# Differential heads of a hybrid block: keys transposed two heads ahead, the last head's steps filled with four blocks' products, two low parts behind the sums, and the last squares summed by TensorE

## The chip, the cores and the metric

The kernel runs on one NeuronCore of one Trainium2 chip. The metric is device time in microseconds of one execution. A NeuronCore has a matrix engine (TensorE, PE in the profile; its weight loads are PEld), a vector engine (VectorE, DVE), a scalar engine (ScalarE, ACT), a general engine (GpSimd, POOL) and a queue engine that issues most transfers (SyncE, SP). Each works through its own list in order and waits for the others by semaphores. SBUF is the on-chip memory, PSUM the memory into which TensorE writes, in eight banks of 128 x 512 fp32.

## The reference

One layer of a streaming encoder on 512 tokens of 1024 features:

```python
h = rms_norm(x, attn_norm_g)
z = h @ w_in                                  # MLA latents | diff q | diff k | diff v
y_mla  = mla_group(...)                       # 8 heads x 64
y_diff = diff_group(...)                      # 4 heads x 128
x = x + concat([y_mla, y_diff], -1) @ w_out
x = x + conv_ffn(rms_norm(x, ffn_norm_g), w_gate, w_up, conv_w, conv_b, w_down)
gate = sigmoid(rms_norm(x, ple_norm_g) @ w_ple_gate)
x = x + gate * (p @ w_ple_proj)
```

A differential head has two softmaxes over 64 features each, with a block-causal mask by chunks of 64 tokens and a bias by distance:

```python
logits = einsum('bhqmd,bhmkd->bhmqk', qb, k_t) * scale + bias   # m = 0, 1; masked
probs  = softmax(logits)
attn   = probs[:, :, 0] - lam * probs[:, :, 1]
o      = rms_norm(attn @ v, out_g) * (1 - lam_init)
```

All arithmetic is fp32.

## The kernel before

**Three products for one.** TensorE multiplies in a reduced format here, so each fp32 operand is split into a high part and a low part, and a product is made of three: high x high, high x low, low x high (`mm3`, lines 152 to 157; in the profile these are the lines 155, 156 and 157). Splitting costs one cast on ScalarE (the high part) and one subtraction on VectorE (the low part) per tile: `split`, lines 180 to 187, for activations; `load_w`, lines 143 to 150, for weights, after a load on SyncE's queue into one of three "raw" buffers.

**Stages around the change.** The MLA heads come first, then the four differential heads (about 160 to 226 us), then the rest of the product with w_out and the sums of squares for the next norm (about 226 to 247 us), then the product p @ w_ple_proj (`pp_unit`, from 242 us on), the normed tokens, and the FFN.

**A differential head `h` in four steps `t`.** Step t works on the queries of tokens 128t to 128t+127. The loop over `dslots` (lines 767 to 782) writes TensorE's order by hand. In each step:
- `diff_logits` two steps ahead: two banks "lg", for m = 0 and 1. VectorE adds the bias and finds the extreme (line 675), ScalarE makes the exponentials and their sums (line 676), VectorE combines both (lines 680 to 682).
- in step 0 only, `diff_T(h + 1, 1)`: the keys of the next head are transposed by TensorE (four transposes, d1T), cast by ScalarE, subtracted by VectorE (`st`).
- `pump(n)`: n units of other work for TensorE, from the list `fill`. `FILL_DIFF` (line 63) says how many in each step of each head. A unit is six products of a block with w_out (two of its eight slices of 128 inputs; `wo_units`, lines 638 to 650). The blocks `b` = 0 to 7 are the eight groups of 128 output features. A block's sum stands in a bank "acc" until VectorE adds it to x (line 631). First come the four MLA slices of all blocks (16 units), then, from head 3 on, slices 4 and 5 (differential heads 0 and 1) of the blocks 0 to 3 (four units).
- `probs_T`: the probabilities are transposed (pTd) and copied by ScalarE (pt, line 541).
- `diff_pv` of the step before: the product with the values (line 690). After step 3 the head's output is squared, summed and scaled (lines 696 to 706: sqo and yd on ScalarE, sso and mo on VectorE, ro on POOL, yd on VectorE).
- in step 0, `diff_T(h + 1, 0)`: the queries of the next head (d0T).
- in step 2, `y_split` of the head before: its output is transposed (yT) and split into yh and yl, the operands of the w_out product.

**Banks.** `bank` gives a PSUM bank by a tag: two "acc", three "lg", two "tp", one "ob". A new user waits until the last reader of the bank's former content is done. All transposes of the heads use "tp".

**After the last head** (lines 783 to 900). Six blocks get what their slices up to 6 still need (lines 802 to 807: one slice for blocks 0 to 3, three for blocks 4 to 7), with the transposes of the last head (`y_split(7)`) ahead of the sixth. Then the loop at 890 adds slice 7 to each in the order 0, 4, 1, 5, 2, 6, 3, 7; the last two blocks are made whole there. Each block is added to x by VectorE and squared by ScalarE; `sums_of` (lines 874 to 885) adds the squares, those of the first four on POOL, the others on VectorE. `norm_r` (lines 909 to 916) sums over the 128 partitions by four products with a column of ones (nr, two passes each) and takes the root; `norm_b` spreads it. `pp_unit` 0 and 1 stand ahead of `norm_r` in TensorE's order, 2 and 3 between `norm_r` and `norm_b`, and 4 to 7 after it. The first token block of the FFN, `tokens`, needs the norm.

**Who sets the order.** TensorE's order is written out in the whole kernel. VectorE's, ScalarE's and POOL's is set by a planner up to line 847: it takes, by its own cost model, what is ready, earlier lines first. `issue_after` holds an instruction behind another one on the same engine: the subtractions of `pk` (line 798) and of the first FFN weights (`behind_head`, lines 833 to 840: wT and wA) stand behind the scaling of the last head. From line 848 on the order of these engines is written out too (`manual_schedule`).

Of the kernel before, what the change touches and what calls it, by code (L numbers as in the profile page):

```python
# [61 lines left out]
FILL_MLA = (1, 1, 1, 1)  # L62
FILL_DIFF = ((2, 1, 1, 1), (1, 1, 2, 1), (1, 2, 2, 1), (1, 1, 2, 2))

# [30 lines left out]
def hybrid_block(ctx: ExitStack, tc: tile.TileContext, a: dict, out: bass.AP):  # L95
# [539 lines left out]
    def wo_w(kq, dq):  # L635
        return load_w(a["w_out"][kq, dq], 1024, f"o{kq}{dq}")
# [14 lines left out]

    df = {}

# [58 lines left out]
    def load_x():  # L712
# [6 lines left out]
        lambda: diff_T(0, 1),  # L719
        lambda: (y_split(0, ymn[0], None, "acc"), y_split(1, ymn[1], None, "acc"), load_x()),  # L720
        lambda: y_split(2, ymn[2], None, "acc"),
# [41 lines left out]
    mla_pv(*slots[-1])  # L763
    diff_logits(0, 1)
    pump()
    y_split(3, ymn[3], None, "tp")
    for i, (h, t) in enumerate(dslots):
        if i + 2 < len(dslots):
            diff_logits(*dslots[i + 2])
        if h + 1 < DH and t == 0:  # L770
            diff_T(h + 1, 1)
        pump(FILL_DIFF[h][t])
        df["pt", h, t] = probs_T(df.pop(("pm", h, t)), t, f"d{h}{t}", True)
        if i:
            diff_pv(*dslots[i - 1])
        if h + 1 < DH and t == 0:
            diff_T(h + 1, 0)
        if h and t == 2:
            y_split(4 + h - 1, df["y", h - 1], ocol, "tp")
        if h and t == 3:  # L780
            if h == 2:
                fill.append(wo_units(1, range(2), 2))
    pump()
    diff_pv(*dslots[-1])
    pump(100)

    for dq in (2, 3):  # L790
        wo2[dq] = wo_w(1, dq)

# [6 lines left out]
    ptw, wpp = (pk[:, 0], pk[:, 1]), [(pk[:, 2], pk[:, 3])]  # L799
    order = (0, 4, 1, 5, 2, 6, 3, 7)  # L800
    early = {}
    for b in order[:6]:
        n = len(early)
        if n == 5:
            y_split(7, df["y", 3], ocol, "tp")
        early[b] = bank("acc" if n < 2 else "lg" if n < 5 else "tp", f"o3{b}")
        mm3(early[b], wo_blocks(6 if b < 4 else 4, 7, b, wo2[b // 2]), True, False)
    att.release()
# [24 lines left out]
    def behind_head(src, tag, name, bufs=1):  # L833

        h_, l_ = (ffn.tile([P, 1024], F32R, tag=tag + j, bufs=bufs, name=f"{tag}{j}{name}") for j in "hl")
        with tc.issue_after(df["copy"].ins):
            df["hi"] = S.copy(h_, src)
        with tc.issue_after(df["scale"].ins):
            df["lo"] = V.tensor_tensor(l_, src, _f32(h_), op=ALU.subtract)
        return h_, l_  # L840

    gu = lambda f, c0, c1: a["w_gu"][f][:, 512 * c0:512 * c1]
    rpp = raw_w(a["w_pp"][1], "rS", "pp1", bufs=3)
    W = {0: {0: behind_head(raw_w(gu(0, 0, 2), "rA", 0, bufs=2), "wA", 0, bufs=2)}}
    wpp.append(behind_head(rpp, "wT", "pp1"))

# [27 lines left out]
    def sums_of(b):  # L874
# [6 lines left out]
        elif 4 < i < 7:  # L881
            V.tensor_tensor(half, half, sq, op=ALU.add)
        elif i == 7:
            V.tensor_tensor(nrm["ss"], nrm["ss"], half, op=ALU.add)
            V.tensor_tensor(nrm["ss"], nrm["ss"], sq, op=ALU.add)

    held = ExitStack()
    for i in ("hi", "lo"):
        held.enter_context(tc.issue_after(df[i].ins))
    for b in order:  # L890
# [3 lines left out]
        else:  # L894
            ps = bank("tp" if b == 3 else "lg", f"o3{b}")
            mm3(ps, wo_blocks(6 if b < 4 else 4, 8, b, wo2[b // 2]), True, True)
        add_x(b, ps)
        sums_of(b)
        held.close()
    wts.release()  # L900

# [7 lines left out]
    def norm_r():  # L909

        ss, ps = nrm["ss"], bank("ob", "nr")
        for t in range(NT):
            TE.matmul(ps[:, t:t + 1], ss[:, tsl[t]], ones[:, :1], start=True, stop=True)
        r4 = sm.tile([P, NT], F32, tag="r4", name="r4")
# [94 lines left out]
    for b in range(2):  # L1009
        pp_unit(b)  # L1010
    norm_r()
    for b in range(2):
        pp_out(b)
# [426 lines left out]
```

## Time and profile before

| what | value |
|---|---|
| median of three runs | 655.68 us (654.13 to 655.93) |
| the profiled execution's own time | 655.36 us |
| its span, first to last instruction | 653.5 us |
| TensorE busy | 642.6 us, 98% of the span |
| VectorE busy | 475.3 us, 73% |
| ScalarE busy | 362.4 us, 55% |
| POOL busy | 57.0 us, 9% |
| mean granted clock of TensorE | 0.995 |

The span is what the trace shows; the execution's own time has 1.86 us more around it. In rows of the trace the form is: start (us), duration (us), engine, line of the kernel, operation, output <- inputs, shapes, number of instructions merged in the row; in brackets the idle time of the engine just before it and what ended that. Durations of products overlap: they are pipelined, so the distance from one start to the next is what one costs. In a row of waits the numbers are the total in us, how many times, and the longest. In a row of a stretch the busy times of PE, PEld, DVE, ACT and POOL follow each other with the number of instructions, then the granted clock of TensorE (1.00 is full), the share of the DMA engines, and GB/s.

### The profile page before, as it was taken

What the parts mean: (1) busy time and instruction counts of PE and PEld (TensorE: products, weight loads), DVE (VectorE), ACT (ScalarE), POOL (GpSimd) and SP (SyncE); (2) the same over time, 40 slices, a digit from 0 to 9 for tenths busy, and PEclk for the clock granted to TensorE, in tenths of its full rate; (3) what the DMA queues carried; (4) which work ended last, traced back from release to release, by engine and by line L of the source; (5) the groups of instructions that cost most, each with busy time, mean ns of one, the idle gap of its engine ahead of it and who ended that gap; (6) DMA issues with size and microseconds to landing.
All of it is one profiled execution on the core that took longest, in us unless ns stands there. A gap on an engine that the chain in (4) does not pass through costs nothing.

```text
span 653.5 us, 10266 instructions
## 1 busy us (share of the span) xinstructions
PE 642.6 (98%) x3932; PEld 569.8 (87%) x3932; DVE 475.3 (73%) x860; ACT 362.4 (55%) x631; POOL 57.0 (9%) x93
## 2 busy tenths in 40 slices
PE   9999999999998999999999999999999999999997
PEld 9988888888777787889999999999999999988886
DVE  6789587666877677888886767677767676759444
ACT  7787666457665445656554645554454545637211
POOL 1520040000000121000100000000001000000000
PEclk9999999999998999999999999999999999999999
DMA  8241224143110157536675646564646464542121
GB/s 308 89 162 46 84 82 161 66 135 123 33 34 2 64 178 241 150 93 172 173 207 136 182 114 178 119 190 128 179 112 178 114 177 113 178 129 62 35 80 49
DMA packets 29912, 82.63 MB, mean 126 GB/s; under 512 B 3100, under 2 KB 4124, under 8 KB 29736
## 3 DMA queue, kind: packets, MB, share of 16 engines
q1 hardware_dynamic: 23816, 69.17, 31.8%
q0 software_dynamic: 5616, 12.33, 10.8%
q8 instruction: 31, 0.51, 0.3%
q10 hardware_dynamic: 432, 0.49, 0.2%
q14 instruction: 17, 0.14, 0.1%
HBM read 77.77 MB, written 5.52 MB: 127 GB/s over the span
## 4 chain that ended last, share of the span: by engine, by line
PE 87%; DVE 6%; ACT 4%; DMA 1%; issue 1%; POOL 0%; ACTq 0%; POOLq 0%
PE dn L157 6%; PE dn L156 6%; PE dn L155 6%; PE gx L157 4%; PE gx L155 4%; PE gx L156 4%; PE g L155 4%; PE g L156 4%; PE g L157 4%; PE zd L155 3%; PE zd L157 3%; PE zd L156 3%; PE pg L155 2%; PE pg L157 2%; PE pg L156 2%; PE u L155 2%
## 5 line engine op out<-in xcount | busy, mean ns | idle before, releaser
L827 DVE TENSOR_TENSOR wSl<-rS,wSh 128x1024 fp32r<-128x1024 f32 x21 | 25.7, 1224 | 44.3 <-ACT wSh L823 44.2
L157 PE MATMUL dn<-ah,lo_dn 128*128 128x512 f32 x144 | 56.4, 392 | 0.0
L156 PE MATMUL dn<-al,hi_dn 128*128 128x512 f32 x144 | 56.3, 391 | 0.0
L155 PE MATMUL dn<-ah,hi_dn 128*128 128x512 f32 x144 | 56.0, 389 | 0.0
L944 POOL DMA_DIRECT2D rS<-in_w_gu x19 | 22.7, 1194 | 251.0 <-DVE cv L1111 138.9
L823 ACT CAST wSh<-rS 128x1024 fp32r<-128x1024 f32 x21 | 22.1, 1051 | 35.6 <-PE gy L156 35.3
L155 PE MATMUL zd<-hi_d,xh 128*128 128x512 f32 x96 | 39.3, 410 | 0.0
L156 PE MATMUL zd<-lo_d,xh 128*128 128x512 f32 x96 | 37.6, 391 | 0.0
L631 DVE TENSOR_TENSOR x<-x,dn 128x512 f32<-128x512 f32 x44 | 29.9, 679 | 6.3 <-PE dn L157 6.1
L827 DVE TENSOR_TENSOR wTl<-rA,wTh 128x1024 fp32r<-128x1024 f32 x19 | 23.3, 1225 | 14.0 <-ACT wTh L823 13.4
L573 ACT ACTIVATE pm<-ml,nm,rq 128x128 f32<-128x128 f32 (+3 forms) x32 | 19.7, 617 | 22.6 <-DVE nm L571 22.6
L157 PEld LDWEIGHTS dn<-ah,lo_dn 128*128 128x128 f32 x144 | 27.0, 188 | 5.7
L156 PEld LDWEIGHTS dn<-al,hi_dn 128*128 128x128 f32 x144 | 27.0, 188 | 5.3
L155 PEld LDWEIGHTS dn<-ah,hi_dn 128*128 128x128 f32 x144 | 27.1, 188 | 5.2
L155 PE MATMUL o<-yh,hi_o 128*128 128x512 f32 x64 | 27.7, 432 | 1.0 <-DVE x L631 1.0
L676 ACT ACTIVATE pmd<-pmd,nmd 128x128 f32<-128x128 f32 (+3 forms) x32 | 17.9, 559 | 17.7 <-DVE nmd L675 17.7
L823 ACT CAST wAh<-rA 128x1024 fp32r<-128x1024 f32 x21 | 22.0, 1050 | 9.7 <-DMA rA<-in_w_gu 9.4
L1114 ACT ACTIVATE cv<-cv 128x512 f32<-128x512 f32 x22 | 13.9, 631 | 23.9 <-DVE cv L1111 23.8
L570 DVE TENSOR_REDUCE nm<-ml 128x1 f32<-128x128 f32 (+3 forms) x32 | 15.6, 487 | 15.1 <-PE ml L157 15.1
L155 PE MATMUL g<-b2h,wAh 128*128 128x256 f32 (+1 forms) x88 | 26.4, 300 | 0.2 <-ACT g L1067 0.2
L156 PE MATMUL g<-b2l,wAh 128*128 128x256 f32 (+1 forms) x88 | 26.2, 297 | 0.0
L157 PE MATMUL g<-b2h,wAl 128*128 128x256 f32 (+1 forms) x88 | 26.2, 297 | 0.0
(467 smaller groups left out, 2226.8 us busy)
## 6 DMA issues: line engine op xcount, KB each, us to landing
rA<-in_w_gu SPq DMA_DIRECT2D x22, 512.0 KB, 3.8
rS<-in_w_gu SPq DMA_DIRECT2D x22, 512.0 KB, 3.6
rS<-in_w_gu POOLq DMA_DIRECT2D x19, 512.0 KB, 6.0
raw_dn<-in_w_down SPq DMA_DIRECT2D x18, 512.0 KB, 5.9
raw_d<-in_w_d SPq DMA_DIRECT2D x12, 512.0 KB, 3.7
r<-in_w_gu SPq DMA_DIRECT2D x19, 256.0 KB, 6.1
raw_o<-in_w_out SPq DMA_DIRECT2D x8, 512.0 KB, 3.7
rS_pg<-in_w_pg SPq DMA_DIRECT2D x6, 512.0 KB, 4.0
```

Source lines behind the costliest of these rows:

```text
L155: TE.matmul(ps, xh, wh, start=first and i == 0, stop=False, skip_group_check=again)
L156: TE.matmul(ps, xh, wl, start=False, stop=False, skip_group_check=again)
L157: TE.matmul(ps, xl, wh, start=False, stop=last and i == n - 1, skip_group_check=again)
L570: V.reduce_max(nm, ps[:, :n], axis=AX.X, negate=True)
L573: S.activation(pm[:, :n], ps[:, :n], AF.Exp, bias=nm, scale=r, accum_out=mla["ssum", h // 2][:, t, h % 2:h % 2 + 1])
L631: V.tensor_tensor(xb(b), xb(b), ps, op=ALU.add)
L676: S.activation(pm[:, :n], pm[:, :n], AF.Exp, bias=nm, scale=-1.0, accum_out=s0 if m == 0 else s1)
L823: S.copy(h_, src)
L827: V.tensor_tensor(l_, src, _f32(h_), op=ALU.subtract)
L944: nc.gpsimd.dma_start(sums[f].rearrange("p (i c) -> p i c", i=2), a["w_gu"][f][:, :2048].rearrange("p (i c) -> p i c", i=2)[:, :, :512], a ...
L1114: S.activation(cv, cv, AF.Silu)
```

## The change

- The keys of head h + 2 are transposed at the end of step 3 of head h; those of head 1 ahead of the first unit, before the loop.
- One unit of head 2 moves from step 2 to step 3. Head 3 pumps 2, 2, 2 and 1 units, and one more comes ahead of its last product. The four units more are slices 4 and 5 of the blocks 4 to 7 (`early_units`), in banks that stay open ("acc" for 4 and 5, "lg" for 6 and 7). The last two pieces of w_out are loaded there, not after the heads.
- After the last head, the blocks 4 to 7 get slice 6, then blocks 0, 1 and 2 are begun with slice 6, with `y_split(7)` behind block 0. The loop that adds slice 7 goes 4, 5, 6, 7, 0, 1, 2, 3; block 3 is made there, in a bank "acc".
- The transposed second MLA block goes through a bank "lg" and not "acc".
- The low parts of wT and wA (one subtraction of 128 x 1024 each on VectorE) are no longer behind the scaling of the last head: that of wT comes after the last sum of squares, that of wA after `norm_r`.
- The last block's squares are not added by VectorE: `norm_r` takes them in four more products with the column of ones, accumulated in the same place.

```diff
-FILL_DIFF = ((2, 1, 1, 1), (1, 1, 2, 1), (1, 2, 2, 1), (1, 1, 2, 2))
+FILL_DIFF = ((2, 1, 1, 1), (1, 1, 2, 1), (1, 2, 1, 1), (2, 2, 2, 1))
...
-    df = {}
+    df, early = {}, {}
+
+    def early_units():
+
+        for b in range(4, 8):
+            if b % 2 == 0:
+                wo2[b // 2] = wo_w(1, b // 2)
+            early[b] = bank("acc" if b < 6 else "lg", f"o3{b}")
+            mm3(early[b], wo_blocks(4, 6, b, wo2[b // 2]), True, False)
+            yield
...
-        lambda: (y_split(0, ymn[0], None, "acc"), y_split(1, ymn[1], None, "acc"), load_x()),
+        lambda: (y_split(0, ymn[0], None, "acc"), y_split(1, ymn[1], None, "lg"), load_x()),
...
     diff_logits(0, 1)
+    diff_T(1, 1)
     pump()
     y_split(3, ymn[3], None, "tp")
     for i, (h, t) in enumerate(dslots):
         if i + 2 < len(dslots):
             diff_logits(*dslots[i + 2])
-        if h + 1 < DH and t == 0:
-            diff_T(h + 1, 1)
         pump(FILL_DIFF[h][t])
         df["pt", h, t] = probs_T(df.pop(("pm", h, t)), t, f"d{h}{t}", True)
         if i:
             diff_pv(*dslots[i - 1])
         if h + 1 < DH and t == 0:
             diff_T(h + 1, 0)
+        if t == 3 and h + 2 < DH:
+            diff_T(h + 2, 1)
         if h and t == 2:
             y_split(4 + h - 1, df["y", h - 1], ocol, "tp")
         if h and t == 3:
             if h == 2:
                 fill.append(wo_units(1, range(2), 2))
+                fill.append(early_units())
     pump()
     diff_pv(*dslots[-1])
     pump(100)
...
-    for dq in (2, 3):
-        wo2[dq] = wo_w(1, dq)
...
-    order = (0, 4, 1, 5, 2, 6, 3, 7)
-    early = {}
-    for b in order[:6]:
-        n = len(early)
-        if n == 5:
+    order = (4, 5, 6, 7, 0, 1, 2, 3)
+    for b in order[:7]:
+        if b < 4:
+            early[b] = bank(("lg", "tp", "ob")[b], f"o3{b}")
+        mm3(early[b], wo_blocks(6, 7, b, wo2[b // 2]), b < 4, False)
+        if b == 0:
             y_split(7, df["y", 3], ocol, "tp")
-        early[b] = bank("acc" if n < 2 else "lg" if n < 5 else "tp", f"o3{b}")
-        mm3(early[b], wo_blocks(6 if b < 4 else 4, 7, b, wo2[b // 2]), True, False)
...
-        with tc.issue_after(df["scale"].ins):
-            df["lo"] = V.tensor_tensor(l_, src, _f32(h_), op=ALU.subtract)
-        return h_, l_
+        return h_, l_, src
...
-    W = {0: {0: behind_head(raw_w(gu(0, 0, 2), "rA", 0, bufs=2), "wA", 0, bufs=2)}}
-    wpp.append(behind_head(rpp, "wT", "pp1"))
+    wA0 = behind_head(raw_w(gu(0, 0, 2), "rA", 0, bufs=2), "wA", 0, bufs=2)
+    W = {0: {0: wA0[:2]}}
+    wT_ = behind_head(rpp, "wT", "pp1")
+    wpp.append(wT_[:2])
...
             V.tensor_tensor(nrm["ss"], nrm["ss"], half, op=ALU.add)
-            V.tensor_tensor(nrm["ss"], nrm["ss"], sq, op=ALU.add)
+            nrm["sq"] = sq
 
     held = ExitStack()
-    for i in ("hi", "lo"):
-        held.enter_context(tc.issue_after(df[i].ins))
+    held.enter_context(tc.issue_after(df["hi"].ins))
     for b in order:
         if b in early:
             ps = early[b]
             mm3(ps, wo_blocks(7, 8, b, wo2[b // 2]), False, True)
         else:
-            ps = bank("tp" if b == 3 else "lg", f"o3{b}")
-            mm3(ps, wo_blocks(6 if b < 4 else 4, 8, b, wo2[b // 2]), True, True)
+            ps = bank("acc", f"o3{b}")
+            mm3(ps, wo_blocks(6, 8, b, wo2[b // 2]), True, True)
         add_x(b, ps)
         sums_of(b)
         held.close()
+    lo_(*wT_)
...
         ss, ps = nrm["ss"], bank("ob", "nr")
+        ss = [ss] + ([nrm.pop("sq")] if "sq" in nrm else [])
         for t in range(NT):
-            TE.matmul(ps[:, t:t + 1], ss[:, tsl[t]], ones[:, :1], start=True, stop=True)
+            for i, s in enumerate(ss):
+                TE.matmul(ps[:, t:t + 1], s[:, tsl[t]], ones[:, :1], start=i == 0, stop=i == len(ss) - 1)
...
     for b in range(2):
         pp_unit(b)
     norm_r()
+    lo_(*wA0)
```

More of the change, by code (lines that the diff above doesn't have):

```diff
@@ L785, in hybrid_block @@
     pump(100)
-    for dq in (2, 3):
-        wo2[dq] = wo_w(1, dq)
+    assert len(early) == 4
     pk = kvp.tile([P, 4, 1024], F32R, tag="kv", name="pk")
```

## The prediction, made before the changed kernel ran

> **What bounds the kernel now.** I read first the page's busy times, then the waits of TensorE, then its order of time wherever it stood idle in the stretch that the diff touches (160 to 260 us), and last the engines it waited for.
>
> ```profile
> span 653.5 us, 10266 instructions
> PE 642.6 (98%) x3932; PEld 569.8 (87%) x3932; DVE 475.3 (73%) x860; ACT 362.4 (55%) x631; POOL 57.0 (9%) x93
> ```
>
> TensorE is busy for 642.6 of 653.5 us, and the diff takes no product away. So the change can only win idle time and slow clock of TensorE. The waits of TensorE between 150 and 265 us (total, times, longest):
>
> ```profile
> PE d0T L657 <- ACT pt L541: 1.7, 1, 1.7
> PE o L155 <- DVE x L631: 1.0, 1, 1.0
> PE yT L617 <- DVE st L184: 0.4, 1, 0.4
> PE nr L913 <- DVE nr L885: 0.4, 1, 0.4
> ```
>
> These four are all there is to win, with one addition, the clock. The stretches in which the longest wait lies and the two that follow (after the engines' busy times: granted clock, DMA share, GB/s), then TensorE's rows in order of time (start, duration):
>
> ```profile
> 198.00:200.00 2.00, 0.93 (x7) 0.73 (x9) 2.00 (x4) 2.00 (x5) 0.00 (x0) 1.00 0.00 0
> 200.00:202.00 2.00, 2.00 (x9) 1.35 (x6) 2.00 (x4) 0.58 (x1) 0.38 (x1) 0.61 0.00 0
> 202.00:204.00 2.00, 2.00 (x6) 1.56 (x5) 1.54 (x5) 0.00 (x1) 0.63 (x1) 0.54 0.00 0
> ```
>
> ```profile
> 199.07 0.66 PE L657 MATMUL d0T<-ident,zd 128*128 128x128 f32 x4 [1.69 <-ACT pt L541]
> ...
> 200.59 0.79 PE L155 MATMUL o<-yh,hi_o 128*128 128x512 f32 x1
> ...
> 204.04 0.39 PE L157 MATMUL o<-yh,lo_o 128*128 128x512 f32 x1
> ...
> 205.98 0.50 PE L155 MATMUL o<-yh,hi_o 128*128 128x512 f32 x1
> ...
> 207.94 0.40 PE L157 MATMUL o<-yh,lo_o 128*128 128x512 f32 x1
> ```
>
> After 1.69 us without work the clock fell to 0.61 and 0.54. From the row at 200.59 to the one at 204.04 it is eight products in 3.45 us; from 205.98 to 207.94 it is eight in 1.96 us. The slow clock cost 3.45 - 1.96 = 1.49 us. This one wait is therefore worth 1.69 + 1.49 = 3.18 us, more than the others together. The wait of 0.96 us at 220 us was followed by no fall.
>
> **Part 1: key transposes earlier.** ScalarE ahead of the wait:
>
> ```profile
> 192.61 1.05 ACT L796 CAST pk<-raw_pp 128x1024 fp32r<-128x1024 f32 x1 [0.53 <-DMA raw_pp<-in_w_pp]
> ...
> 197.35 0.56 ACT L183 CAST st<-d1T 128x512 fp32r<-128x512 f32 x1
> 197.81 1.04 ACT L148 CAST hi_o<-raw_o 128x1024 fp32r<-128x1024 f32 x1
> 198.76 0.26 ACT L541 COPY pt<-pTd 128x128 f32<-128x128 f32 x1
> ```
>
> The query transpose d0T of head 3 needs one of the two "tp" banks; the copy of pTd that frees it stood behind the cast of the keys d1T, whose bank was the other one, and behind a weight cast. The change issues the keys one step earlier (end of step 3 of the head before), so that bank is read out before d0T asks for it. Nothing is added: the same four transposes, cast and subtraction. The wait should go, and the clock with it: -3.18 us; bounds 0 (the weight cast at 197.81, 1.04 us long, still stands ahead of the copy that is needed) and -3.18. I take the whole, because d0T no longer needs the late bank. For head 1 the keys now go ahead of the transposes of the fourth MLA block, whose low part is used soon after; at the same place the second MLA block takes an "lg" bank, which aims at the 0.4 us wait on st. Gain and loss there are each bounded by that row, 0.4 us; I take 0.
>
> **Part 2: filling the last head.** Head 2 spreads its units so that step 3 has one, and head 3 gets seven units and an eighth ahead of its last product, where it had four. Products are moved, not added. Their weights cost nothing new: the loads of all eight w_out pieces were issued long before (below, SyncE's queue), ahead of the pT load as now, and the last cast of them is the row at 197.81. The cover is this distance of some 20 us to the units; without it a load and a cast would stand in the step.
>
> ```profile
> 144.95 11.95 SPq L140 DMA_DIRECT2D raw_o<-in_w_out  x3
> 175.61 0.33 SPq L140 DMA_DIRECT2D raw_pT<-in_pT  x1
> ```
>
> The wait to be won here, VectorE first, then TensorE:
>
> ```profile
> 219.30 0.69 DVE L706 TENSOR_TENSOR yd<-yd,ro 128x512 f32<-128x512 f32 x1 [0.57 <-POOL ro L704]
> 219.91 0.68 DVE L631 TENSOR_TENSOR x<-x,o 128x512 f32<-128x512 f32 x1
> ```
>
> ```profile
> 220.64 0.50 PE L155 MATMUL o<-yh,hi_o 128*128 128x512 f32 x1 [0.96 <-DVE x L631]
> ```
>
> A unit waited for its "acc" bank, whose addition stood in VectorE's queue behind the scaling that waited for POOL. Four w_out blocks and two of the new ones still go through the two "acc" banks, in steps 0 to 2. So it is between 0 and -0.96. I take -0.7, nearer to the row: the addition was late through one scaling in the queue, and in the new order the bank that is asked for at that time was filled a step earlier.
>
> **Part 3: what the moved products covered.** They stood behind the last head product and hid the chain that makes the last head's y. TensorE, ScalarE, VectorE in order of time:
>
> ```profile
> 225.67 0.48 PE L155 MATMUL o<-yh,hi_o 128*128 128x512 f32 x1
> ...
> 231.91 0.60 PE L617 MATMUL yT<-ident,yd 128*128 128x128 f32 x4
> 232.26 0.47 PE L155 MATMUL o<-yh,hi_o 128*128 128x512 f32 x1
> ```
>
> ```profile
> 232.54 0.69 ACT L186 ACTIVATE yh<-yT,ocol 128x512 fp32r<-128x512 f32 x1 [5.51 <-PE yT L617]
> ```
>
> ```profile
> 228.65 0.69 DVE L706 TENSOR_TENSOR yd<-yd,ro 128x512 f32<-128x512 f32 x1 [1.19 <-POOL ro L704]
> 229.26 1.22 DVE L798 TENSOR_TENSOR pk<-raw_pT,pk 128x1024 fp32r<-128x1024 f32 x1
> 230.39 1.22 DVE L798 TENSOR_TENSOR pk<-raw_pp,pk 128x1024 fp32r<-128x1024 f32 x1
> 233.27 0.75 DVE L187 SCALAR_TENSOR_TENSOR yh7l<-yT,ocol,yh 128x512 fp32r<-128x512 f32 x1 [1.66 <-ACT yh L186]
> ```
>
> The 27 products from 225.67 to 231.91 give 6.24 / 27 = 0.231 us each. y is ready at 228.65 + 0.69 = 229.34, 3.67 us after 225.67. The new order leaves 15 products, 3.47 us: +0.2 us of waiting. The transposes then run from about 229.4 and hold TensorE for 232.26 - 231.91 = 0.35 us; six products (1.39) follow, so the first product with yh7 comes at 231.14 and the one with its low part at 231.37. But VectorE is in the two pk subtractions until 230.39 + 1.22 = 231.61, and the low part takes 0.75 more: 232.36, a wait of 0.99. If the planner puts it between them it is ready 233.27 - 231.91 + 0.75 = 2.11 us after the transposes start, 231.51: a wait of 0.14. The pk subtractions come first in the program and are ready first; I take +0.8.
>
> **Part 4: the sums of squares.** The subtractions of wT and wA leave the front of this stretch, the last square goes to TensorE. VectorE, ScalarE, TensorE:
>
> ```profile
> 240.90 0.82 DVE L882 TENSOR_TENSOR nr<-nr,nsq 128x512 f32<-128x512 f32 x1 [0.75 <-ACT nsq L878]
> 241.64 0.67 DVE L631 TENSOR_TENSOR x<-x,o 128x512 f32<-128x512 f32 x1
> 243.08 0.69 DVE L882 TENSOR_TENSOR nr<-nr,nsq 128x512 f32<-128x512 f32 x1 [0.76 <-ACT nsq L878]
> 243.69 0.68 DVE L631 TENSOR_TENSOR x<-x,o 128x512 f32<-128x512 f32 x1
> ```
>
> ```profile
> 244.46 0.63 ACT L878 ACTIVATE nsq<-x 128x512 f32<-128x512 f32 x1 [1.42 <-DVE x L631]
> ```
>
> ```profile
> 245.12 0.39 PE L157 MATMUL pp<-pk 128*128 128x512 f32 x1
> 245.87 1.05 PE L913 MATMUL nr<-ones,nr 128*128 128x1 f32 x8 [0.37 <-DVE nr L885]
> 246.79 0.48 PE L155 MATMUL pp<-pk 128*128 128x512 f32 x1
> ```
>
> Here the order is written out, so each block goes: add, square on ScalarE, add of the square. From one such add to the next is 243.08 - 240.90 = 2.18 us, add to add of the square 243.08 - 241.64 = 1.44, add of the square to the next block's add 0.61 to 0.74. Let T be when TensorE leaves the sixth block; its add starts some 0.28 us later (the lag from 232.26 to 232.54). Then the square is added at T + 1.72, the seventh at T + 3.90, the eighth block's add starts at T + 4.51 and ends at T + 5.13, its square ends at T + 4.51 + 0.77 + 0.63 = T + 5.91. TensorE has after T now only the seventh block (3 products), the eighth (6) and pp0 (6): T + 3.47. And pp1 takes an "acc" bank: with two of them, and block 3 now in "acc" too, pp1's is block 3's, free at T + 5.13. TensorE waits 5.13 - 3.47 = 1.66 us, and behind pp1 are the norm's products and everything else of TensorE. Lower bound 1.2, if the sixth block's add is not behind. In exchange the norm's own wait goes, which is 245.87 - (245.12 + 0.23) = 0.52: net +1.14. The eight 128x1 passes take 246.79 - 245.87 = 0.92 us; sixteen cost +0.92, none of it hidden, since TensorE is the bound. The moved subtractions, 1.2 us each on VectorE, lie one behind the sums while TensorE does pp1, one behind the norm's scaling while TensorE does pp2 to pp7; without these products the second would delay the first token block by its 1.2 us.
>
> **Sum.** -3.18 + 0 - 0.7 + 0.2 + 0.8 + 1.14 + 0.92 = -0.82 us. The profiled run took 655.36 us, 1.86 more than its span; that gives 654.5. The runs' median is 655.68, 0.32 above the profiled run; I predict 654.7.
>
> **Rivals.** (a) *All waits of the heads go and the tail costs its lower bounds.* For it: the bounds are read off an order in which VectorE was late. Against: the written order forces the chain. -3.18 - 0.96 - 0.4 + 0.2 + 0.14 + (1.2 - 0.52) + 0.92 = -2.6: 652.9.
> (b) *The clock falls in the tail.* The wait for pp1's bank, 1.66 us, is as long as the 1.69 that cost 1.49 us, and the sixteen narrow passes follow. Against: 0.96 us at 220 us brought no fall, and the wait is shorter than the one that did. -0.82 + 1.49 = +0.67: 656.2.
> [...]
> (c) *Slower: the long wait stays.* Place: d0T of head 3. Mechanism: ScalarE runs in order and still waits for the raw_pp load (0.53 us at 192.61), casts it (1.05), and casts the weights (1.04) ahead of the copies and casts that free the two "tp" banks. [...] Then the 3.18 stay in: -0.82 + 3.18 = +2.36: 657.9. For it: those casts are untouched. Against: one of the three items in front of the copy, the key cast of 0.56 us, is gone, and the bank needed is another.
>
> **How the numbers follow.** Forecast 0.45, (a) 0.28, (b) 0.17, (c) 0.10. What a measurement can tell from no change is about 0.3%, 1.97 us: faster means under 653.7, slower over 657.65. Faster takes most of (a), 0.23, and 0.08 of the forecast: 0.31. Slower takes half of (c) and a little of (b): 0.08. Same 0.61. The range runs from a little below (a), where the first bounds all fall well, to a little above (b): 652.3 to 656.8; the forecast's own is 653.4 to 655.9.
>
> **What would show it.** Right: no 1.7 us wait of d0T and a full clock from 195 to 210 us; a wait of pp on VectorE's x (1.2 to 1.7 us) right before the norm; nr with sixteen passes and no wait; a wait of some 0.8 us on yh7l. Wrong: a PEclk below 1 in the stretch of the norm (b), a d0T that waits for pt or st (c), or a pp1 that starts with no wait, which would break my reading of the "acc" banks.

## The result and the profile after

The kernel with the change takes 662.18 us (661.63 to 662.46, median of 4), the kernel before 655.54 us beside it (654.13 to 655.93, median of 4). The ratio is 1.0101 with an interval of [1.0074, 1.0128]: some 6.6 us slower. The prediction was 654.7 us in a range of 652.3 to 656.8, with a chance of 0.08 for slower. It was wrong.

The profiled execution of after took 662.22 us. Its page begins:

```profile
span 660.4 us, 10291 instructions
PE 647.9 (98%) x3940; PEld 574.5 (87%) x3940; DVE 475.6 (72%) x859; ACT 363.0 (55%) x631; POOL 56.6 (9%) x93
```

TensorE has only eight instructions more, the eight narrow passes of the norm, but 5.3 us more of busy time (642.6 before), and its idle time rose from 10.9 to 12.5 us. Most of the loss is therefore time with products in it, slower ones above all. The waits of TensorE from 150 to 280 us in after (total, times, longest) show where the idle time went:

```profile
PE pp L155 <- DVE x L631: 2.8, 1, 2.8
PE pTm L538 <- ACT pm L573: 0.9, 1, 0.9
PE o L156 <- DVE yh7l L187: 0.6, 1, 0.6
PE dl L157 <- DVE st L187: 0.4, 1, 0.4
PE o L155 <- DVE x L631: 0.3, 1, 0.3
PE yT L617 <- DVE yd L715: 0.2, 1, 0.2
```

The wait of d0T (1.7 us before) is gone, as forecast. The largest wait is now the one for the bank of pp1, the second product of p @ w_ple_proj. The stretches of after around it (busy times of PE, PEld, DVE, ACT, POOL, then granted clock, DMA share, GB/s):

```profile
244.00:248.00 4.00, 1.24 (x6) 0.73 (x5) 3.25 (x5) 1.00 (x2) 0.35 (x1) 1.00 0.01 5
248.00:252.00 4.00, 4.00 (x20) 3.74 (x18) 1.28 (x2) 2.17 (x4) 0.00 (x0) 0.61 0.42 63
252.00:256.00 4.00, 4.00 (x13) 3.28 (x13) 2.18 (x4) 0.49 (x2) 2.28 (x2) 0.54 0.52 200
256.00:260.00 4.00, 4.00 (x17) 2.92 (x16) 3.64 (x5) 2.34 (x5) 0.00 (x0) 1.00 1.04 211
```

The clock falls behind that wait; 0.61 and 0.54 are means over 4 us. In before every stretch from 240 to 256 us had 1.00. TensorE in order of time, after (start, duration; in brackets the wait):

```profile
243.28 0.40 PE L155 MATMUL pp<-pk 128*128 128x512 f32 x1
...
247.59 0.50 PE L155 MATMUL pp<-pk 128*128 128x512 f32 x1 [2.76 <-DVE x L631]
...
248.62 0.40 PE L156 MATMUL pp<-pk 128*128 128x512 f32 x1
248.84 0.60 PE L157 MATMUL pp<-pk 128*128 128x512 f32 x1
249.24 0.42 PE L924 MATMUL nr<-ones,nr 128*128 128x1 f32 x2
...
252.51 0.77 PE L155 MATMUL pp<-pk 128*128 128x512 f32 x1
...
263.18 0.39 PE L155 MATMUL g<-b1h,wAh 128*128 128x512 f32 x1
```

The last product ahead of the norm's passes, at 248.84, is already slow: the next row comes 0.40 us later, where the one before had 0.22.

Call the time from the first product of pp0 to the first product g of the FFN the norm's stretch: 263.18 - 243.28 = 19.90 us here. In before the same two landmarks lie at 242.57 and 255.97 us: 13.40. This stretch alone lost 6.50 us; the heads ahead of it did not pay for it.

**What of the 6.9 us between the two spans is the change.** The order of instructions is the same in both kernels up to about 145 us, and yet in this profile the three issues of raw_o, the last common point, start at 147.38 us and not at 144.95. The 2.43 us arise at the start: the sixteen one-column passes ssx, sums for the first norm, begin 0.73 us later than in a later profile of the same kernel (20.73 against 20.00 us), and some 1.6 us more are lost behind them, where the clock fell. After's stretch, then the same stretch in that later profile (e13):

```profile
24.00:28.00 4.00, 4.00 (x16) 3.88 (x15) 3.00 (x14) 2.03 (x5) 3.08 (x8) 0.63 0.35 112
```

```profile
24.00:28.00 4.00, 4.00 (x22) 3.67 (x21) 3.61 (x24) 3.18 (x5) 3.12 (x12) 1.00 0.29 100
```

So this part belongs to the execution and not to the change. To separate the two, both kernels were profiled again, unchanged.

> The changed kernel once more. Theory 'chance at the start': the slow clock at 24 to 28 us and the first loads that land 0.9 us late are not of this program; some of these executions lack them and take 1.5 to 2.4 us less than 662.2. Rival 'of the program': all of them lie between 661.6 and 662.5 again. The slow clock behind the norm (249 to 255 us) should be in most of them.

It took 662.72 us (662.1 to 663.96, 4 executions), ratio 1.0107 [1.0088, 1.0126], and repeats the result.

> The changed kernel, one look. Chance: the first loads land early or late, and the clock at 20 to 28 us is 1.0 or about 0.65, independent of the program. Of the program: late loads and a slow clock at 24 to 28 us again, as in both looks so far. Behind the norm (248 to 256 us) the clock about 0.5 either way.

> As the look before it: the changed kernel once more, for the same question.

> The kernel before, one look. Chance: the start may show late loads and a slow clock at 24 to 28 us here too, and the slow clock behind d0T's wait at 200 us may be missing. Of the program: the start is at full clock, as in its one look so far.

> As the look before it: the kernel before once more, for the same question.

The change took 661.50 and 661.48 us, before 653.48 and 653.67 us, one execution each; in none of the four did the clock fall at the start. e13 (the change) and e14 (before) are compared here. TensorE's rows in order of time, e13 first:

```profile
240.92 0.40 PE L155 MATMUL pp<-pk 128*128 128x512 f32 x1
...
245.24 0.63 PE L155 MATMUL pp<-pk 128*128 128x512 f32 x1 [2.76 <-DVE x L631]
...
262.39 0.39 PE L155 MATMUL g<-b1h,wAh 128*128 128x512 f32 x1
```

```profile
241.02 0.40 PE L155 MATMUL pp<-pk 128*128 128x512 f32 x1
...
244.31 1.05 PE L913 MATMUL nr<-ones,nr 128*128 128x1 f32 x8 [0.36 <-DVE nr L885]
...
245.23 0.48 PE L155 MATMUL pp<-pk 128*128 128x512 f32 x1
...
254.41 0.39 PE L155 MATMUL g<-b1h,wAh 128*128 128x512 f32 x1
```

At pp0 the change is level with before (240.92 against 241.02). The norm's stretch takes 21.47 us against 13.39. The whole difference of the spans, 659.7 - 651.7 = 8.0 us, is made in this stretch, and e13 has the fall of the clock there as well. It begins with the first product behind the wait (the six of pp1 lie 0.43 us apart), 2.4 us ahead of the norm's first pass at 247.81:

```profile
242.04:245.45 3.41, 0.65 (x3) 0.21 (x3) 2.65 (x5) 0.80 (x2) 0.00 (x0) 1.00 0.00 0
245.45:248.86 3.41, 3.41 (x12) 2.83 (x11) 1.48 (x2) 2.47 (x4) 0.00 (x0) 0.50 0.36 25
```

For all kernels below, the norm's stretch from the starts of the same two products (us):

| profile | pp0 | first g | norm's stretch |
|---|---|---|---|
| before | 242.57 | 255.97 | 13.40 |
| before (e14) | 241.02 | 254.41 | 13.39 |
| after | 243.28 | 263.18 | 19.90 |
| after (e13) | 240.92 | 262.39 | 21.47 |
| e1, keys alone | 240.98 | 254.38 | 13.40 |
| e2, block 3 elsewhere | 243.36 | 262.45 | 19.09 |
| e3, VectorE adds the last squares | 240.80 | 256.92 | 16.12 |
| e4, keys as before | 243.74 | 265.19 | 21.45 |
| e5, more products ahead of the norm | 243.39 | 260.03 | 16.64 |
| e6, last squares alone | 241.49 | 255.17 | 13.68 |
| e7, keys, fill, wT | 239.35 | 252.58 | 13.23 |
| e8, low parts alone | 241.20 | 255.31 | 14.11 |
| e9, additions first | 240.96 | 255.48 | 14.52 |
| e10, without POOL's sums | 242.57 | 258.46 | 15.89 |

### The profile page after: what moved, and what is told of

Same layout as the page of the kernel before. It is cut to its first block, busy times and chain, and to the rows that moved or that the text cites. A ratio compares the mean times of both kernels' runs of the same rounds, so it can differ in the third digit from the quotient of the medians.

```text
span 660.4 us, 10291 instructions
## 1 busy us (share of the span) xinstructions
PE 647.9 (98%) x3940; PEld 574.5 (87%) x3940; DVE 475.6 (72%) x859; ACT 363.0 (55%) x631; POOL 56.6 (9%) x93
## 4 chain that ended last, share of the span: by engine, by line
PE 81%; DVE 8%; ACT 5%; DMA 3%; issue 2%; POOL 0%; ACTq 0%; POOLq 0%; DVEq 0%; SPq 0%
PE dn L157 6%; PE dn L156 6%; PE dn L155 6%; PE gx L157 4%; PE gx L155 4%; PE gx L156 4%; PE g L155 4%; PE g L157 4%; PE g L156 4%; PE zd L155 3%; PE zd L157 3%; PE zd L156 3%; PE pg L155 2%; PE pg L157 2%; PE pg L156 2%; PE u L156 2%
## 5 line engine op out<-in xcount | busy, mean ns | idle before, releaser
L836 DVE TENSOR_TENSOR wAl<-rA,wAh 128x1024 fp32r<-128x1024 f32 x22 | 26.8, 1217 | 1.2 <-ACT wAh L832 1.0
```

## The experiments

**The key transposes, alone on before (e1) and alone taken out of after (e4).** The edit of e1; e4 is the same edit undone:

```diff
     diff_logits(0, 1)
+    diff_T(1, 1)
     pump()
...
-        if h + 1 < DH and t == 0:
-            diff_T(h + 1, 1)
...
+        if t == 3 and h + 2 < DH:
+            diff_T(h + 2, 1)
```

> The kernel before with one part of the change alone: the key transposes two heads ahead. Theory 'tail' (the loss of the change sits behind the heads; this part wins): the 1.69 us wait of d0T and the slow clock behind it go, 655.5 - 3.2 = 652.3 us. Rival 'heads' (moving transposes only moves the wait, because ScalarE's order is replanned): within 0.5 us of 655.5, with a wait of about 1 to 2 us elsewhere between 160 and 225 us.

> The change with the key transposes where they were before. Theory 'tail': the keys are the part that wins, so without it d0T waits again for 1 to 1.7 us, and if the clock falls there too the time is 662.2 + 1.7 to 3.2 = 664 to 665.4 us. Rival 'heads': the same or less than 662.2 us. The start of the kernel (the first 150 us) has the same order of instructions in all of these kernels: if the slow clock at 24 to 28 us of the changed profile belongs to chance, some of them show it and some do not.

With the keys alone 653.61 us (653.32 to 655.74, 10 executions) against 654.72 (653.40 to 657.07, 13): ratio 0.999 [0.9979, 1.0001]. The wait of d0T is gone, but the gain is at most about 1.4 us by the interval, not 3.18. The other direction shows why: e4 (662.1 us, 1.0118 [1.0094, 1.0142]) has the wait again, and no fall of the clock behind it. Its wait, then its stretch:

```profile
PE d0T L666 <- ACT pt L541: 1.8, 1, 1.8
```

```profile
200.00:204.00 4.00, 2.53 (x15) 1.79 (x16) 3.93 (x9) 2.98 (x6) 0.00 (x0) 1.00 0.00 0
```

Before itself, in e14 and e15, has the wait of d0T (1.8 and 1.7 us) with a full clock behind it as well. Of six profiles with this wait (before, e4, e6, e8, e14, e15) only the one from which the prediction was made has the fall. It is not of the program. The executions of before beside e1 with a mean clock of 1.0 took 653.87 to 654.72 us, those with 0.995 took 654.93 to 657.07; where it was lower in these, a mean doesn't say.

The wait itself was not won whole either. From raw_o to pp0 e1 takes 95.51 us, the four profiles with before's order there and a full clock (e6, e8, e14, e15) 95.92 to 96.28: 0.4 to 0.8 us less, though a wait of 1.7 to 1.8 us is gone. The only new wait is one of 0.2 us (dl for st). What took the rest is open.

**The bank of pp1: block 3 elsewhere (e2).**

```diff
-            ps = bank("acc", f"o3{b}")
+            ps = bank("tp", f"o3{b}")
```

> The change with block 3 in a bank tp instead of acc, so that pp1 need not wait for block 3's addition. Theory 'bank': the 2.76 us wait of pp1 goes and the clock stays up: 662.2 - 2.8 - 3 = about 656.5 us. Rival 'chain of sums': TensorE comes to the norm's passes at about 246.1 us on the time axis of the changed profile, while the last square ends at 248.3; a wait of about 2.2 us stands there instead, and the time falls by only 0.5 us, to about 661.7, with the slow clock still there.

658.55 us (657.43 to 661.55, 4), 1.0068 [1.0041, 1.0095]. The wait of pp1 is gone, so the bank was read rightly. But TensorE then waits at the norm, for the same chain of sums:

```profile
PE nr L924 <- DVE nr L893: 2.0, 1, 2.0
```

```profile
248.00:252.00 4.00, 3.72 (x17) 3.72 (x18) 1.52 (x3) 2.26 (x4) 0.03 (x1) 0.56 0.41 58
```

The bank only decides where the wait stands; VectorE's chain of additions and sums is what is late. The clock falls here too (0.56). This profile is of the slowest of the four executions; the two fastest, 657.43 and 657.88 us, had a mean clock of 0.996 and 0.997 and not its 0.991.

**More products ahead of the norm (e5).** As e2, with four products of pp ahead of the norm's first step where there are two, and two ahead of its second:

```diff
-    for b in range(2):
+    for b in range(4):
         pp_unit(b)
     norm_r()
```

> The change with block 3 in a bank tp, and in TensorE's order pp0 to pp3 ahead of the norm's products, pp4 and pp5 ahead of the spreading, pp6 and pp7 behind it. Theory 'cover' (the loss is the cover of products taken from the chain of sums, and the slow clock follows from that wait): in the run with only the bank changed TensorE came to the norm 1.40 us after pp1's start plus 2.0 us of waiting; two more products sets give 2.7 us, so no wait and no slow clock there; from the first pp to the first g about 14 us, not 19 to 20; 658.5 - 4 = about 654.5 us. Rival 'only moved': the token blocks come later behind the norm, and TensorE waits 1 to 2 us on them at its first g products: about 656.5 us. Rival 'sixteen narrow passes pull the clock down by themselves': a clock of about 0.5 for 3 us behind the norm all the same.

658.6 us (658.26 to 660.91, 6), 1.0055 [1.0035, 1.0076]. TensorE no longer waits at the norm and its clock stays at 1.00 from 244 to 260 us. The norm's stretch falls from 19.90 to 16.64 us and not to 13.4: the first FFN product waits instead. Its bank is free when ScalarE's last copy of pp ends (259.40, 0.58 us), and that copy stands among the casts of the normed tokens, which begin only at 256.84 (252.10 in before).

```profile
PE g L155 <- ACT ppo L947: 2.8, 1, 2.8
```

**Eight passes instead of sixteen (e3).** The last squares are added by VectorE again, all else as in after:

```diff
-            nrm["sq"] = sq
+            V.tensor_tensor(nrm["ss"], nrm["ss"], sq, op=ALU.add)
```

> The change with the last block's squares added by VectorE again, so that the norm has eight narrow passes and not sixteen. Theory 'narrow passes pull the clock down': the clock stays at 1.0 behind the norm, 662.2 - 0.9 - 3 = about 658 us. Rival 'the wait pulls it down': the 2.76 us wait of pp1 stays, the clock falls all the same, and only the eight passes are saved at the slow clock, 8 x 0.21 = 1.7 us: about 660.5 us.

659.17 us (658.31 to 660.96, 4), 1.008 [1.006, 1.0099]. The wait of pp1 is the same, a wait of 0.8 us for the tokens' b2h is new, and the clock does not fall in its profile:

```profile
PE pp L155 <- DVE x L631: 2.7, 1, 2.7
```

```profile
248.00:252.00 4.00, 4.00 (x17) 3.00 (x16) 3.07 (x4) 2.12 (x3) 0.90 (x1) 1.00 0.93 274
```

That the missing eight passes kept the clock up is not shown by this: in after and e13 the fall began before the first pass, and the part on rival (b) below finds another difference. Two of e3's four executions had a mean clock of 1.0 (658.31 and 658.40 us), the others 0.997 and 0.991 (659.95 and 660.96 us), and 0.991 is what after's profile has; at which place it was lower in these, a mean doesn't say. What is left against before, 16.12 us in the stretch, is the wait.

**The sixteen passes alone (e6) and the low parts alone (e8), both on before.** e6 keeps the last squares for TensorE:

```diff
-            V.tensor_tensor(nrm["ss"], nrm["ss"], sq, op=ALU.add)
+            nrm["sq"] = sq
```

> The kernel before with one part alone: the last block's squares summed by TensorE, sixteen narrow passes and not eight. Theory 'price of the passes': eight more cost 0.92 us and the norm's wait of 0.52 goes: +0.4 us, about 655.1. Rival 'narrow passes pull the clock down': the clock falls behind the norm in most runs, +2 to +3 us, about 657.5.

655.09 us (653.68 to 657.36, 12), 0.9997 [0.9982, 1.0012]: no difference. The norm's wait of 0.4 us goes, the passes take 1.70 us where they took 0.92, and the clock stays full:

```profile
244.00:248.00 4.00, 4.00 (x27) 3.56 (x26) 0.73 (x2) 2.21 (x5) 1.62 (x2) 1.00 0.34 131
```

e8 moves only the two low parts behind the sums:

```diff
-        with tc.issue_after(df["scale"].ins):
-            df["lo"] = V.tensor_tensor(l_, src, _f32(h_), op=ALU.subtract)
...
+    lo_(*wT_)
     wts.release()
...
     norm_r()
+    lo_(*wA0)
```

> The kernel before with one part alone: both low parts (wT, wA) behind the sums. Theory 'sums start earlier': the norm's wait of 0.52 us goes, about 654.2. Rival 'tokens late': the subtraction of wA ahead of the first token block delays it by 1.2 us, and TensorE waits on b2h or b2l in its first g products, as in the run with the vector sum (0.8 us and more): 654.7 to 656.

655.86 us (654.6 to 657.73, 12), 1.001 [0.9995, 1.0024]: not told apart from no change. The norm's wait did not go, it is 0.8 us (0.4 in before). The trace shows something that no step of the prediction had. VectorE, then POOL, in order of time:

```profile
239.02 1.75 DVE L882 TENSOR_TENSOR nr<-nr,nsq 128x512 f32<-128x512 f32 x1 [1.01 <-ACT nsq L878]
```

```profile
237.57 2.66 POOL L880 TENSOR_TENSOR nr<-nr,nsq 128x512 f32<-128x512 f32 x2 [0.24 <-ACT nsq L878]
```

VectorE's first sum of a square takes 1.75 us, where in before it took 0.82. It runs into the last of POOL's additions to the other half of the sums, and ends 0.54 us after POOL does (240.77 against 240.23). In after it is the same: VectorE, then POOL, whose two additions end at 244.35 and the sum of VectorE at 244.90, 0.55 us later.

```profile
243.13 1.77 DVE L891 TENSOR_TENSOR nr<-nr,nsq 128x512 f32<-128x512 f32 x1 [1.01 <-ACT nsq L887]
244.82 0.67 DVE L631 TENSOR_TENSOR x<-x,o 128x512 f32<-128x512 f32 x1
```

```profile
241.68 2.67 POOL L889 TENSOR_TENSOR nr<-nr,nsq 128x512 f32<-128x512 f32 x2 [0.23 <-ACT nsq L887]
```

**Without POOL's additions (e10).** From after, with the line of POOL taken out; so the squares of the second to fourth block are left out of the norm.

```diff
-            G.tensor_tensor(nrm["ss"], nrm["ss"], sq, op=ALU.add)
+            pass
```

> The change without POOL's three additions of squares (the squares of the second, third and fourth block are left out of the norm). Theory 'shared access' (VectorE's sum of the sixth square took 1.77 us in the changed profile, since POOL adds at that time; without it, 0.69): the wait of pp1 falls from 2.76 to about 1.7 us, which is what my forecast had for it. Rival: the 1.77 us has another cause, and the wait stays at 2.7 us. The slow clock may or may not follow from 1.7 us.

659.61 us (657.76 to 662.78, 5), 1.0058 [1.0035, 1.0081]. The sum takes 0.69 us again and the wait of pp1 is 1.7 us, near the 1.66 that the prediction had worked out:

```profile
PE pp L155 <- DVE x L631: 1.7, 1, 1.7
```

```profile
242.42 0.69 DVE L891 TENSOR_TENSOR nr<-nr,nsq 128x512 f32<-128x512 f32 x1 [1.01 <-ACT nsq L887]
```

So the 1.1 us by which the wait is longer in after come from POOL. The clock stayed full in this profile.

**The additions to x ahead of the sums (e9).** After, with VectorE adding the last three blocks to x first and their sums of squares behind:

```diff
-            V.tensor_tensor(half, half, sq, op=ALU.add)
+            nrm.setdefault("late", []).append(sq)
...
         elif i == 7:
+            for s in nrm.pop("late"):
+                V.tensor_tensor(half, half, s, op=ALU.add)
```

> The change with one thing moved: VectorE adds the sixth, seventh and eighth block to x first, and adds their squares after that (the same instructions, another order). Theory 'chain on VectorE' (block 8's addition is late because each addition stands behind the sum of the square before it): pp1's bank is free in time, no wait of 2.8 us; the norm waits at most 0.5 us; no slow clock there; from the first pp to the first g about 14 us, not 19.9. The token blocks may then be waited for, 1 to 2 us, as in the run with the vector sum. About 655 to 656.5 us. Rival 'bank': as long as block 3 is in acc, pp1 waits some 2 us whatever VectorE's order, about 661 us.

656.51 us (655.9 to 658.24, 12), 1.0018 [1.0005, 1.0031]. No wait of pp1, 0.3 us at the norm, a full clock, and the sixteen passes in 246.02 - 244.21 = 1.81 us:

```profile
244.21 0.38 PE L926 MATMUL nr<-ones,nr 128*128 128x1 f32 x2 [0.33 <-DVE nr L895]
...
246.02 0.48 PE L155 MATMUL pp<-pk 128*128 128x512 f32 x1
```

The norm's stretch is 14.52 us. Another order of VectorE's additions gives back most of the 6.6 us: 1.0018 against 1.0101. So the wait of pp1 and the slow clock behind it are what made the change slow. The stretch is still 1.1 us longer than in before; the sixteen passes (1.81 against 0.92) are 0.89 of it.

**The keys and the fill, with less moved (e7).** e1, with the distribution of units over the steps as the change has it in head 2 and one unit per step in head 3, no blocks 4 to 7 in the heads, and only the low part of wT behind the sums:

```diff
-FILL_DIFF = ((2, 1, 1, 1), (1, 1, 2, 1), (1, 2, 2, 1), (1, 1, 2, 2))
+FILL_DIFF = ((2, 1, 1, 1), (1, 1, 2, 1), (1, 2, 1, 1), (1, 1, 1, 1))
...
+    lo_(*wT_)
     wts.release()
```

> A version put together: the kernel before with the keys two heads ahead, one unit in every step of the last head and one in step 3 of head 2 (no early units, no new order behind the heads), and only the low part of wT behind the sums. Theory: the 0.96 us wait on x at 220 us and the norm's 0.52 go beside the wait of d0T: about 653.6 - 1.4 = 652.2 us. Rival: the wait on x moves by a step and the token blocks set the end: no better than the keys alone, 653.6.

652.12 us (651.54 to 654.33, 11), 0.9958 [0.9942, 0.9973]: 0.4% faster than before, and faster than after. Its waits from 150 to 300 us are all short:

```profile
PE yT L617 <- DVE st L184: 0.4, 1, 0.4
PE dl L157 <- DVE st L187: 0.4, 1, 0.4
PE pTm L538 <- ACT pm L573: 0.2, 1, 0.2
PE nr L917 <- DVE nr L888: 0.2, 1, 0.2
```

Both long waits of before, d0T and o, are gone; the products that cover the chain of the last head's y stay behind the heads, and the norm's stretch is 13.23 us, as short as in before (13.40).

## Why the prediction was wrong, by its own steps

**Where the sum failed first: the keys, -3.18.** The wait went, as forecast. The term had added 1.49 us of slow clock from one profile; that fall did not come in the five other profiles with the same wait. The wait of 1.69 us was real, but less than half of it was won: measured alone the keys gave 0.65 us by the ratio of e1 (interval from a gain of 1.4 to a loss of 0.1), and 0.4 to 0.8 us between raw_o and pp0.

**Waits of the heads: in part.** The wait on x went from 1.0 to 0.3 us, as taken (-0.7). yT waits 0.2 us, as taken. The wait on yh7l is 0.6 us, taken 0.8. The second MLA block in a bank "lg" was taken as 0; the wait of yT on st (0.4 us in before) did go, but pTm now waits 0.9 us for pm (0.2 us in e14) and dl 0.3 for st in e13. These two new waits, 1.0 us, have no term in the sum; that of pTm stands in e4 too, so it is not the keys'. With the slow clock and these corrected, the terms up to pp0 add to -1.8 - 0.7 + 0.2 + 0.6 - 0.4 + 1.0 = -1.1 us; between e13 and e14, from raw_o (144.98 and 144.74) to pp0 (240.92 and 241.02), it is 95.94 - 96.28 = -0.3. The remaining 0.8 us are not explained by a wait, as in e1.

**The wait for pp1's bank, 1.66: right mechanism, wrong size.** It is 2.76 us. The chain of additions was followed rightly to the bank, but the duration of the sum, 0.69 us, was taken from a row of before (243.08) at which POOL had finished. (The row at 243.69 takes 0.68 us and the prediction counted 0.62 for it; that makes 1.72.) The sum ahead of it met POOL's additions in before too. POOL's second and third:

```profile
239.88 1.29 POOL L880 TENSOR_TENSOR nr<-nr,nsq 128x512 f32<-128x512 f32 x1
241.25 1.62 POOL L880 TENSOR_TENSOR nr<-nr,nsq 128x512 f32<-128x512 f32 x1
```

VectorE's sum began at 240.90, 0.27 us before POOL's second addition ended (241.17), and took 0.82 us; POOL's third came behind it and took 1.62 where the others took 1.29. In after VectorE's sum began at 243.13, just behind the start of POOL's third addition (243.06), met all of it and took 1.1 us longer; the bank depends on it. VectorE's sum ends 0.54 and 0.55 us after POOL's addition in e8 and after, and 0.55 in before (241.72 against 241.17); in e10, without POOL, it takes 0.69 us.

That the low parts' move alone brings the later meeting shows in e8 (1.75 us), which has no other edit. By what step it does so is open: ScalarE's cast of wAh (1.03 us at 239.97 in after) now stands in the middle of the squares that both engines wait for, but a kernel with that cast elsewhere was not tried.

**Sixteen passes, +0.92: right.** 0.89 us with a full clock (1.81 in e9 against 0.92).

**Rival (b), the clock falls in the tail: it is what happened, with a chance of 0.17 and a price of 1.49.** Both were too low, and of the steps that failed this is the largest; without it the change would still be 8.0 - 4.6 = 3.4 us slower between e13 and e14. In e13 the norm's stretch is 8.08 us longer than in e14. The distance from pp0 to pp1 grew by 2.93 us (4.32 against 1.39 in e14), the norm's wait of 0.36 is gone, and sixteen passes cost 0.89: together 3.46. The other 4.6 us are the slow clock. In the first profile of after the same reckoning is 6.50 - 2.91 + 0.37 - 0.89 = 3.1 us. The prediction priced it from one fall of 3.4 us; here the clock was at half speed for 6.8 us in after and 10.2 in e13. And its argument against, that the wait is shorter than the one that brought the fall, fell: the wait was 2.76 us.

Behind which waits the clock fell can be set beside the times of its changes. In after these lie whole multiples of 3.413 us apart: it falls at 23.59, returns at 27.00, falls at 248.86, which is 66 times 3.413 us after the first fall, and returns at 255.69, two times later. In before it falls at 200.44 and returns at 203.86, one time later. The stretches below are cut in these steps, from a profile's own changes; where none of its changes is near, the steps are continued, which is the author's estimate. After's from the wait on, then e3's two that share its wait:

```profile
245.45:248.86 3.41, 1.27 (x6) 1.06 (x7) 2.65 (x5) 1.86 (x3) 0.00 (x0) 1.00 0.00 0
248.86:252.28 3.42, 3.42 (x17) 3.33 (x16) 0.42 (x1) 1.31 (x3) 0.00 (x0) 0.50 0.57 107
252.28:255.69 3.41, 3.41 (x10) 2.73 (x11) 1.87 (x3) 0.18 (x1) 2.28 (x2) 0.50 0.52 201
255.69:259.10 3.41, 3.41 (x15) 2.44 (x14) 3.07 (x4) 1.95 (x3) 0.00 (x0) 1.00 0.95 153
```

```profile
240.03:243.45 3.42, 2.33 (x11) 1.55 (x9) 2.36 (x2) 0.93 (x3) 1.74 (x2) 1.00 0.33 128
243.45:246.86 3.41, 1.76 (x9) 1.37 (x9) 2.95 (x5) 1.99 (x4) 0.00 (x0) 1.00 0.00 0
```

TensorE stood idle for 3.41 - 1.27 = 2.14 us of after's first stretch, and the clock fell at its end. In e3 a wait of 2.74 us is cut by an edge, 1.1 us on one side and 1.65 on the other, and the clock did not fall. The table has, for the stretch that holds most of the wait, the time that TensorE waited in it and the time in it that went to passes of one column (us):

| profile, place | stretch | waited | narrow passes | clock behind |
|---|---|---|---|---|
| e13, pp1 | 242.04 to 245.45 | 2.76 | 0 | 0.50 |
| e12, pp1 | 242.20 to 245.61 | 2.75 | 0 | 0.50 |
| e4, pp1 | 244.80 to 248.21 | 2.74 | 0 | 0.50 |
| e11, pp1 | 245.23 to 248.64 | 2.49 | 0 | 0.50 |
| after, pp1 | 245.45 to 248.86 | 2.14 | 0 | 0.50 |
| e2, norm | 245.09 to 248.50 | 1.99 | 0.22 | 0.50 |
| after, start (ssx) | 20.17 to 23.59 | 0.23 | 1.78 | 0.50 |
| e3, pp1 | 243.45 to 246.86 | 1.65 | 0.27 | 1.00 |
| e10, pp1 | 244.18 to 247.60 | 1.63 | 0.29 | 1.00 |
| e14, d0T | 195.79 to 199.21 | 1.84 | 0 | 1.00 |
| e5, first g | 255.62 to 259.03 | 1.81 | 0 | 1.00 |
| e6, norm | 242.67 to 246.08 | 0 | 1.70 | 1.00 |
| before, d0T | 197.03 to 200.44 | 1.69 | 0 | 0.50 |

In the rows with a fall, wait and narrow passes together come to 2.01 us (after's start) to 2.76 us, but for the last row; in the rows with a full clock behind them to 1.70 to 1.92 us. The last row, the wait of d0T in before, has 1.69 us and a fall; why it fell there and not in e14, with 1.84 us, is open. In e4 and e6, by the same steps, an edge cuts the wait of d0T (in e6 the wait lies from 197.69 to 199.50 us, the edge at 198.30). In after, e11, e12 and e13 the stretch ahead of the fall holds the wait of pp1 and no narrow pass; the passes stand behind the fall. The clock was then slow for two stretches in after and e2, for three in e4, e11, e12 and e13, for one in before and at the start of after. The last slow stretch holds 0.23 us of passes in after and none in e11 and e13; in e11 the one ahead of it holds 0.90 us. At the start of after a fall stands behind 1.78 us of passes of ssx and 0.23 us of wait. All this is read from the traces side by side; no run moved the edges on purpose, so what makes the clock fall or return is not shown.

**Part 3, what the moved products covered: the terms right, the consequence behind them too small.** The two terms, +0.2 and +0.8, came as 0.2 and 0.6 us. But with these products gone from behind the heads VectorE's additions and sums of eight blocks have only 3.47 us of TensorE's work beside them once the sixth block is left. The prediction saw it as the wait of pp1 alone. Of the ways out of it that were tried, a bank of its own moves the wait to the norm (e2), more products ahead of the norm move it to the first FFN product (e5), and another order of VectorE's additions removes it (e9).

**The other rivals.** (a), 652.9 with the heads' waits all gone and a cheap tail, did not come; e7, which leaves the products where they covered the chain, is near that time (652.12). (c), the wait of d0T stays, fell: it is gone in after and e1. Its sum counts 1.49 us of slow clock with the wait, which the profile of before alone shows; behind waits of d0T of 1.65 to 1.84 us the clock stayed full in the five other profiles that have one.

## What to carry to other kernels

A slow clock seen once in a profile is not a term of a sum: look for it in a second profile before counting its end as a gain. Nor is a wait that goes a gain of its whole length: e1 lost a wait of 1.7 us and won 0.4 to 0.8. Products moved off the end of a stage take the cover from whatever runs beside them; before moving them, count the chain of the other engine from its first late instruction, and check each of its durations for a neighbour (here POOL) that it did not meet before. Price a new wait with the clock behind it: the wait of 2.76 us was followed by a slow clock that cost another 3.1 us in after and 4.6 us in e13 by the reckoning above, and e9, with VectorE's additions in another order, has neither the wait nor the fall.

## What the runs showed of the hardware that was not expected

- Two engines adding in SBUF: VectorE's sum of 128x512 fp32 takes 0.69 us alone. When it begins while POOL's addition runs, it ends 0.54 or 0.55 us after that: 0.82 us when it met the last 0.27 us of it (before), 1.75 to 1.77 when it met nearly all (e8, after). POOL's addition takes 1.29 to 1.30 us, and 1.62 behind VectorE's.
- The changes of the granted clock lie whole multiples of 3.413 us apart in after (23.59, 27.00, 248.86 and 255.69 us) and in before (200.44 and 203.86 us). Of the stretches in the table, those with 2.01 to 2.76 us of waiting and one-column passes were followed by half speed, those with 1.70 to 1.92 us by full clock, and before's, with 1.69 us at d0T, by half speed.
- Behind the wait of pp1 the slow clock lasted two or three such stretches and cost 3.1 and 4.6 us where it was reckoned, more than the wait itself.
- The clock at the start can fall at 23 to 27 us in one execution and not in another of the same program; with the later start of ssx it made 2.4 us between two profiles of after. In the five profiles with this fall SyncE's last issue of the first weight's load comes at 8.6 to 9.0 us, in e13 at 7.88; what made it late is open, and it is not enough, since e10 has it at 9.68 and no fall.
